# The residual of a one-core mLSTM / attention / expert block: loaded a second time and added by VectorE, and its products for the expert sums moved into the third expert group

## The chip, the cores and the metric

The kernel is one program on one core of a Trainium2 chip. The metric is the device time of one execution in microseconds (us), from a few timed runs; beside it stands one execution that the hardware profiler recorded, with its own time and its span (first to last instruction). TensorE is PE in the profile, VectorE DVE, ScalarE ACT, GpSimd POOL, SyncE SP. Each engine works through its own list of instructions in order and waits for others by semaphores.

## The reference

256 tokens of 1024 numbers go through one block: a mixer (an mLSTM group and a differential attention group), then 32 experts of which each token uses two, then a last norm. What matters here are the two residual sums:

```python
def reference(x, w_in, ..., w_out, norm1_g, norm2_g, ..., w_eg, w_eu, w_ed, normf_g):
    h = rmsnorm(x, norm1_g[l])
    proj = h @ w_in[l]
...
    x = x + jnp.concatenate([y_m, y_d.astype(x.dtype)], axis=-1) @ w_out[l]
    h2 = rmsnorm(x, norm2_g[l])
    x = x + hier_moe(h2, w_rg[l], b_rg[l], w_re[l], b_re[l], w_eg[l], w_eu[l], w_ed[l])
    return rmsnorm(x, normf_g)
```

`hier_moe` picks a group and two experts in it for each token by the logits of h2, and adds `gates * ((silu(t @ w_eg) * (t @ w_eu)) @ w_ed)` over the experts. The sum after `w_out` is called x1 below.

## The kernel before, in words

**Stages.** The first 150 us compute the mixer: projections with `w_in`, the recurrence, the attention, then the product with `w_out`, the router's logits and the list of experts. From there on the kernel runs ten groups of experts (a fixed four, then pairs and fours in the order of their load), `for pr in range(LAST)` at L1028, and one last group by hand. The expert weights are 32 x 6 MB in pieces of 1 MB.

**Weights and their places.** `order` lists 23 places (slots) of 1 MB in turn: six that the mixer also uses (`wa`), eleven that open when the mixer's tiles are closed (`wbs`, after `bx.close()`), six more at the other end of the memory (`wzs`). `load` (L877) sends a group's pieces on SP's queue; a piece waits until its slot's last reader is done, which for the first round means the mixer's tiles that lay there, and for the eighth transfer before it. From the seventh piece of `w_ed` on, a piece's expert is read out of `permi`, the order of the experts by load, which is known only when the router is done.

**The accumulators.** `acc[j][t]` are four banks of PSUM of 512 columns, j for the half of the 1024 columns and t for the half of the tokens. They take x1 and then all expert results (`scatter`, L845), and are read by the last norm.

**The stage around the change.** With `acc` open, TensorE first multiplies the residual into it, by the identity (L573 to L575):

```python
for j in range(2):
    for t in range(NT):
        T.matmul(acc[j][t], ident, xs[:, t, j * 512:(j + 1) * 512], start=True, stop=False, skip_group_check=True)
```

`xs` is x as the kernel loaded it at the start, one tile under the slots `wbs`. Then come eight steps k with three products for each half of the tokens: `wh` and `wl` are the high and the low part of a 128-row piece of `w_out`, made by ScalarE (L232) and VectorE (L233); `yH` and `yL` are those of the mixer's output (L566 and L567 for the mLSTM half, from `tm`, L565; L533 and L534 for the attention half). `cols` cuts the 1024 columns into blocks of 512, 256 and 256. Out of every 256 columns (a quarter, i) the kernel makes `x1` in the on-chip memory (L621, copies out of `acc`, one by VectorE and one by ScalarE), its squares (L628), its transposes (L638, L640) and the router's products (L647), whose logits VectorE adds up in `lg` (L652, L654). `keep_x1` (L592) keeps x1 for the experts' gathers in `x1c`, in an order (k, q) of the columns that fits the experts' weights.

What stands in which order on an engine is set by a scheduler with a timeline model of its own; `issue_after` and `high_priority` are hints to it.

Of the kernel before, what the change touches and what calls it, by code (L numbers as in the profile page):

```python
# [10 lines left out]
F32 = mybir.dt.float32  # L11
# [5 lines left out]
OP = mybir.AluOpType  # L17
AX = mybir.AxisListType

P = 128  # L20
S = 256
NT = 2
D = 1024
KD = 8
# [80 lines left out]
def kernel(ctx: ExitStack, tc: tile.TileContext,  # L105
# [467 lines left out]
    for j in range(2):  # L573
        for t in range(NT):
            T.matmul(acc[j][t], ident, xs[:, t, j * 512:(j + 1) * 512], start=True, stop=False, skip_group_check=True)  # L575

# [15 lines left out]
    def keep_x1(j, after):  # L592

        with tc.issue_after(after.ins):
            for t in range(NT):
                A.copy(x1c[:, t, :, j * 64:(j + 1) * 64],
                       acc[j][t].rearrange("p (q k) -> p k q", k=KD))
# [3 lines left out]
    for b, (c0, nc_) in enumerate(cols):  # L601
# [6 lines left out]
        for n, k in enumerate((4, 5, 6, 7, 0, 1, 2, 3) if b else (4, 5, 0, 1, 2, 3, 6, 7)):  # L608
            wh, wl = split(wo[2 * j + 1 - k // 4][:, k % 4, cs], rooms[n % 4] if b else two(n))
            for t in range(NT):  # L610
                ts = slice(t * P, (t + 1) * P)
                T.matmul(po[t], yH[:, k, ts], wh, start=False, stop=False, skip_group_check=True)  # L612
                T.matmul(po[t], yL[:, k, ts], wh, start=False, stop=False, skip_group_check=True)  # L613
                T.matmul(po[t], yH[:, k, ts], wl, start=False, stop=(n == KD - 1), skip_group_check=True)  # L614
        for i in range(c0 // 256, (c0 + nc_) // 256):
# [3 lines left out]
            x1 = px1.tile([P, NT, 256], F32, name="x1", tag="x1", bufs=2)  # L619
            for t in range(NT):  # L620
                (A.copy if t else V.tensor_copy)(x1[:, t], po[t])  # L621
# [33 lines left out]
            if i == 1:  # L655
                keep_x1(0, ev)
    keep_warm(NW2, pw, pe)
    if dbg is not None:
        for j in range(2):
            for t in range(NT):  # L660
                SY.dma_start(dap(dbg, t * P * D + j * 512, [[D, P], [1, 512]]), x1[j][:, t])
# [8 lines left out]
    keep_x1(1, behind[0])  # L670
# [174 lines left out]
    def scatter(n, S_, oj, j, stop=False):  # L845
        for o_ in halves(n, oj):
            for t in range(NT):
                T.matmul(acc[j][t], S_[:n, t * P:(t + 1) * P], o_[:n], start=False, stop=stop, skip_group_check=True)  # L848
# [182 lines left out]
    for pr in range(LAST):  # L1031
# [6 lines left out]
        for j, oj in enumerate(down(ws, hT, [po2(), po2()])):  # L1038
            scatter(P, S_, oj, j)
# [168 lines left out]
```

## Time and profile before

| | us |
|---|---|
| median of 3 runs | 592.17 (590.98 to 594.12) |
| the profiled execution's own time | 594.47 |
| its span | 592.7 |
| PE, DVE, ACT, POOL busy in it | 517.1, 158.2, 122.5, 9.4 |
| mean granted clock of TensorE | 0.955 of full speed |
| moved by DMA | 223.76 MB, mean 378 GB/s |

The profiled execution took 2.3 us more than the median of the runs, and its span leaves 1.8 us of its own time outside. Times of the trace count from the start of the span. A busy PE is not PE at its peak, since products that follow each other overlap in the records; the distance between two starts is the better measure there.

### The profile page before, as it was taken

To read this page: it belongs to the slowest core of one execution; us is meant where nothing else is said; L and a number is where in the kernel's file an instruction comes from. 1 tells how busy PE (TensorE), PEld (TensorE's weight loads), DVE (VectorE), ACT (ScalarE), POOL (GpSimd) and SP (SyncE) were. 2 spreads that over 40 slices of the span, in tenths; PEclk is the share of its full clock that TensorE was granted. 3 is DMA by queue.
4 is the path that set the end of the run, shared out by engine and by line. 5 is a ranking of instruction groups with operands and counts; after the bars stand their busy time and mean duration, and the time that the engine had idled before them with its cause. 6 is when DMAs were issued, how large, how long until landed. Compare 5 with 4: busy or idle time off the path is not lost.

```text
span 592.7 us, 7989 instructions
## 1 busy us (share of the span) xinstructions
PE 517.1 (87%) x3004; PEld 263.5 (44%) x3004; DVE 158.2 (27%) x463; ACT 122.5 (21%) x287; POOL 9.4 (2%) x19
## 2 busy tenths in 40 slices
PE   8999999999969999799897897995897986885783
PEld 6898879796353343334242252341243331221130
DVE  3784688946031120201102002001002002000022
ACT  4775568663011000000100000000010000000032
POOL 0000002201000000000000000000000000000000
PEclk9999999999969999999799998999999989899798
DMA  8964799998999999999999999999999999999991
GB/s 292 390 190 112 225 387 382 322 343 346 388 420 417 421 417 421 419 418 421 419 420 418 421 418 421 419 419 420 420 420 420 419 420 419 420 419 421 399 346 73
DMA packets 49019, 223.76 MB, mean 378 GB/s; under 512 B 3796, under 2 KB 6228, under 8 KB 27348
## 3 DMA queue, kind: packets, MB, share of 16 engines
q1 hardware_dynamic: 48692, 222.89, 94.6%
q8 instruction: 24, 0.39, 0.3%
q10 hardware_dynamic: 288, 0.35, 0.2%
q14 instruction: 15, 0.12, 0.1%
HBM read 221.39 MB, written 1.84 MB: 377 GB/s over the span
## 4 chain that ended last, share of the span: by engine, by line
PE 48%; DMA 46%; DVE 3%; ACT 1%; issue 1%; SPq 0%; ACTq 0%
DMA w<-in_w_ed_dram 18%; DMA w<-in_w_eu_dram 17%; PE pmm L906 11%; DMA w<-in_w_eg_dram 10%; PE pmm L923 7%; PE pmm L815 4%; PE pj L264 3%; PE pj L261 3%; PE pj L263 3%; PE acc L848 1%; PE pj L274 1%; PE pj L275 1%; PE acc L612 1%; PE pj L273 1%; PE acc L613 1%; PE acc L614 1%
## 5 line engine op out<-in xcount | busy, mean ns | idle before, releaser
L906 PE MATMUL pmm<-w,xg 128*32 128x512 f32 (+1 forms) x1024 | 189.8, 615 | 24.2 <-DMA w<-in_w_eu_dram 16.0
L906 PEld LDWEIGHTS pmm<-w,xg 128*32 128x32 f32 (+1 forms) x1024 | 47.0, 118 | 139.1 <-issue 89.9
L923 PE MATMUL pmm<-w,oL 128*32 128x512 f32 (+1 forms) x448 | 93.9, 673 | 11.8 <-ACT oL L835 6.1
L923 PEld LDWEIGHTS pmm<-w,oL 128*32 128x32 f32 (+1 forms) x448 | 27.9, 130 | 72.2 <-issue 45.9
L233 DVE TENSOR_TENSOR wl<-w,wh 128x512 fp32r<-128x512 f32 (+1 forms) x72 | 44.5, 629 | 24.4 <-ACT wh L232 21.7
L842 DVE TENSOR_TENSOR oL<-pmm,oH 128x512 fp32r<-128x512 f32 x18 | 12.4, 691 | 134.3 <-PE pmm L923 111.3
L815 PEld LDWEIGHTS pmm<-Gm,x1c 128*128 128x128 f32 x320 | 39.9, 204 | 16.5 <-issue 8.9
L815 PE MATMUL pmm<-Gm,x1c 128*128 128x128 f32 x320 | 43.0, 293 | 4.7 <-DVE beg L997 4.7
L232 ACT ACTIVATE wh<-w 128x512 fp32r<-128x512 f32 (+1 forms) x72 | 41.0, 581 | 29.5 <-PE pj L263 13.7
L263 PE MATMUL pj<-hL,wh 128*128 128x256 f32 x128 | 36.9, 292 | 0.0
L261 PE MATMUL pj<-hH,wh 128*128 128x256 f32 x128 | 36.2, 294 | 0.0
L264 PE MATMUL pj<-hH,wl 128*128 128x256 f32 x128 | 36.1, 293 | 0.0
L835 ACT COPY oL<-pmm 128x512 f32<-128x512 f32 x9 | 5.3, 586 | 139.0 <-PE pmm L832 139.0
L841 ACT CAST oH<-pmm 128x512 fp32r<-128x512 f32 x18 | 10.6, 586 | 112.8 <-PE pmm L923 92.7
L816 DVE TENSOR_TENSOR xg<-pmm,cb 128x512 f32<-128x512 f32 (+1 forms) x22 | 13.5, 639 | 68.3 <-PE pmm L906 51.9
L263 PEld LDWEIGHTS pj<-hL,wh 128*128 128x128 f32 x128 | 25.1, 196 | 0.1
L264 PEld LDWEIGHTS pj<-hH,wl 128*128 128x128 f32 x128 | 24.5, 195 | 1.4 <-issue 1.2
L261 PEld LDWEIGHTS pj<-hH,wh 128*128 128x128 f32 x128 | 24.7, 196 | 0.2
L832 PE MATMUL pmm<-ca,oH 128*128 128x128 f32 x40 | 6.9, 300 | 18.7 <-DVE oH L828 18.7
L913 ACT ACTIVATE oL<-pmm,rg 128x512 f32<-128x512 f32 x9 | 6.2, 688 | 80.3 <-PE pmm L906 62.9
L832 PEld LDWEIGHTS pmm<-ca,oH 128*128 128x128 f32 x40 | 4.7, 152 | 26.1 <-issue 23.6
L613 PE MATMUL acc<-wh,yL 128*128 128x256 f32 (+1 forms) x48 | 15.1, 322 | 0.0
(337 smaller groups left out, 476.0 us busy)
## 6 DMA issues: line engine op xcount, KB each, us to landing
w<-in_w_eu_dram SPq DMA_DIRECT2D x64, 1024.0 KB, 19.8
w<-in_w_eg_dram SPq DMA_DIRECT2D x64, 1024.0 KB, 19.8
w<-in_w_ed_dram SPq DMA_DIRECT2D x56, 1024.0 KB, 19.8
w<-in_w_in_dram SPq DMA_DIRECT2D x10, 1024.0 KB, 14.6
w<-in_w_ed_dram SPq DMA_DIRECT2D x12, 512.0 KB, 13.6
w<-in_w_out_dram SPq DMA_DIRECT2D x4, 1024.0 KB, 12.8
w<-in_w_ed_dram SPq DMA_DIRECT2D x8, 256.0 KB, 7.4
w<-in_w_in_dram SPq DMA_DIRECT2D x3, 512.0 KB, 8.2
```

Of the source, the lines that this page charges most:

```text
L232: A.activation(wh, raw, AF.Copy)
L233: V.tensor_tensor(wl, raw, wh.bitcast(F32), op=OP.subtract)
L261: T.matmul(om, wh[:, cs], hH[:, k], start=(k == 0 and m % 2 == 0), stop=False, skip_group_check=True)
L263: T.matmul(om, wh[:, cs], hL[:, k], start=False, stop=False, skip_group_check=True)
L264: T.matmul(om, wl[:, cs], hH[:, k], start=False, stop=(k == KD - 1), skip_group_check=True)
L613: T.matmul(po[t], yL[:, k, ts], wh, start=False, stop=False, skip_group_check=True)
L815: gat_end[0] = T.matmul(px_[:, i * P:i * P + n], x1c[:, t, k0 + i], G_[:, t], start=(t == 0), stop=(t == NT - 1))
L816: V.tensor_tensor(xg[:, k0:k0 + per, :n], px_.rearrange("p (k s) -> p k s", k=4)[:, :per, :n], cb[:, B_N2 + k0:B_N2 + k0 + per, None].to_b ...
L832: T.transpose(pt[:, k * P:k * P + n], hid[:n, k], ident[:n, :n])
L842: V.tensor_tensor(oL[:n], oj[:n], oH[:n].bitcast(F32), op=OP.subtract)
L906: up_end[0] = T.matmul(p_[i * cap:(i + 1) * cap], xg[:, k, i * cap:(i + 1) * cap], of(ws, n_, i, k), start=(k == 0), stop=(k == KD - 1))
L923: down_end[0] = T.matmul(ojs[j][i * cap:(i + 1) * cap], hT[:, k, i * cap:(i + 1) * cap], ws["d", i, k // 2][:, c0:c0 + 512], start=(k == 0 ...
```

## The change

The four products of the residual into `acc` are gone; the first product of `w_out` now starts each bank. Each quarter of x comes from memory a second time, 256 KB by a DMA on GpSimd's queue, into the tile that `x1` uses (two of them in turn; the third load waits until the first quarter is used up). VectorE adds the bank to it, for both halves of the tokens. `keep_x1` now copies each quarter out of `x1` rather than each half out of `acc`. As `acc` holds no residual any more when the experts begin, the first group's first product starts it anew, and behind the third group's scatters (`pr == 2`) four products of `x1c` with the identity bring x1 in.

```diff
     acc = [[pacc.tile([P, 512], F32, name=f"acc{j}{t}") for t in range(NT)] for j in range(2)]
-    for j in range(2):
-        for t in range(NT):
-            T.matmul(acc[j][t], ident, xs[:, t, j * 512:(j + 1) * 512], start=True, stop=False, skip_group_check=True)
-
     bx.close()
...
-    def keep_x1(j, after):
+    def keep_x1(i, x1, after):
 
         with tc.issue_after(after.ins):
             for t in range(NT):
-                A.copy(x1c[:, t, :, j * 64:(j + 1) * 64],
-                       acc[j][t].rearrange("p (q k) -> p k q", k=KD))
+                A.copy(x1c[:, t, :, i * 32:(i + 1) * 32], x1[:, t].rearrange("p (q k) -> p k q", k=KD))
+
+    def load_x1(i):
+
+        x1 = px1.tile([P, NT, 256], F32, name="x1", tag="x1", bufs=2)
+        G.dma_start(x1, dap(x, i * 256, [[D, P], [P * D, NT], [1, 256]]))
+        return x1
+
+    x1s = [load_x1(i) for i in range(2)]
...
-                T.matmul(po[t], yH[:, k, ts], wh, start=False, stop=False, skip_group_check=True)
+
+                T.matmul(po[t], yH[:, k, ts], wh, start=(n == 0 and cj == 0), stop=False, skip_group_check=True)
...
-            x1 = px1.tile([P, NT, 256], F32, name="x1", tag="x1", bufs=2)
+            x1 = x1s[i]
             for t in range(NT):
-                (A.copy if t else V.tensor_copy)(x1[:, t], po[t])
+                V.tensor_tensor(x1[:, t], x1[:, t], po[t], op=OP.add)
...
-            if i == 1:
-                keep_x1(0, ev)
+            if not last:
+                keep_x1(i, x1, ev)
+                if i < 2:
+                    x1s.append(load_x1(i + 2))
...
-    keep_x1(1, behind[0])
+    keep_x1(3, x1s[3], behind[0])
...
+    def residual():
+
+        for j in range(2):
+            for t in range(NT):
+                T.matmul(acc[j][t], ident, x1c[:, t, :, j * 64:(j + 1) * 64].rearrange("p k q -> p q k"),
+                         start=False, stop=False, skip_group_check=True)
...
         for j, oj in enumerate(down(ws, hT, [po2(), po2()])):
-            scatter(P, S_, oj, j)
+            scatter(P, S_, oj, j, pr == 0)
+        if pr == 2:
+            residual()
```

The scheduler also moves other instructions. On VectorE, in the first block of `w_out` (`tm`, `yL` are the mixer's output, `wl` the low part of `w_out`, `cT` the mLSTM's output before its gate, `l` the attention's), before:

```order
L565 TENSOR_TENSOR tm<-cT,zs 128x256 x2
L522 TENSOR_SCALAR l<-pm,rso 128x128 x4
L567 TENSOR_TENSOR yL<-tm,yH 128x256 x2
L565 TENSOR_TENSOR tm<-cT,zs 128x256
L233 TENSOR_TENSOR wl<-w,wh 128x512
L567 TENSOR_TENSOR yL<-tm,yH 128x256
L550 SCALAR_TENSOR_TENSOR cT<-pm,ca,cT 128x256
```

and now:

```order
L565 TENSOR_TENSOR tm<-cT,zs 128x256 x2
L522 TENSOR_SCALAR l<-pm,rso 128x128 x4
L233 TENSOR_TENSOR wl<-w,wh 128x512
L550 SCALAR_TENSOR_TENSOR cT<-pm,ca,cT 128x256
L567 TENSOR_TENSOR yL<-tm,yH 128x256
L233 TENSOR_TENSOR wl<-w,wh 128x512
L567 TENSOR_TENSOR yL<-tm,yH 128x256
L534 SCALAR_TENSOR_TENSOR yL<-pm,ca,yH 128x512
L565 TENSOR_TENSOR tm<-cT,zs 128x256 x2
L233 TENSOR_TENSOR wl<-w,wh 128x512
L567 TENSOR_TENSOR yL<-tm,yH 128x256
L233 TENSOR_TENSOR wl<-w,wh 128x512
```

The first two `yL` stood right behind L522 and the third one four rows later; now two and four rows come ahead of the first two, and nine operations behind L522 ahead of the third. On VectorE in the third quarter (`x_1642` before and `x_1555` now are its `x1`, `lg` the router's logits of the quarters ahead of it), before:

```order
L652 COPY lg<-pm 128x80
L621 COPY x_1642<-acc_1397 128x256
L233 TENSOR_TENSOR wl<-w,wh 128x256
L654 TENSOR_TENSOR lg<-lg,pm 128x80
L640 COPY x1T<-pm 128x256
```

and now:

```order
L656 COPY lg<-pm 128x80
L233 TENSOR_TENSOR wl<-w,wh 128x256
L658 TENSOR_TENSOR lg<-lg,pm 128x80
L625 TENSOR_TENSOR x_1555<-x_1555,acc_1397 128x256
L625 TENSOR_TENSOR x_1555<-x_1555,acc_1398 128x256
L644 COPY x1T<-pm 128x256
```

The third quarter's `x1` now stands behind the addition of the second quarter's logits, and it is two rows of VectorE where one was VectorE's and one ScalarE's. On SP, where the list of experts is first read (`TENSOR_LOAD permi` brings an expert's number into a register of SP), before:

```order
L770 DMA w<-in_w_ed_dram 128x2048 x6
L768 TENSOR_LOAD permi
L768 ISA x2
L770 DMA w<-in_w_ed_dram 128x2048
L768 TENSOR_LOAD permi
L768 ISA x2
L770 ISA
L770 DMA w<-in_w_eg_dram 128x2048
```

and now:

```order
L772 DMA w<-in_w_ed_dram 128x2048 x6
L770 TENSOR_LOAD permi
L770 ISA x2
L770 TENSOR_LOAD permi
L770 ISA x2
L772 DMA w<-in_w_ed_dram 128x2048
L770 TENSOR_LOAD permi
L770 ISA x2
L770 TENSOR_LOAD permi
L770 ISA x2
L772 ISA
L772 DMA w<-in_w_eg_dram 128x2048
```

Two reads stand ahead of the next transfer where one stood, and two more ahead of the one behind it.

## Rows read from the trace of the kernel before

**Rows 1.** Chain that ended last: start, us, what; its last transfer.

```profile
558.49 9.06 DMA w<-in_w_ed_dram
```

**Rows 2.** Stretches: us; PE, PEld, DVE, ACT, POOL busy; clock; DMA share; GB/s.

```profile
104.00:110.00 6.00, 5.83 (x34) 4.19 (x34) 5.67 (x18) 4.46 (x11) 4.04 (x5) 1.00 0.68 219
...
130.00:138.00 8.00, 7.60 (x66) 7.45 (x65) 3.12 (x9) 4.32 (x13) 0.00 (x0) 1.00 0.66 198
...
150.00:152.00 2.00, 2.00 (x27) 0.53 (x19) 0.00 (x0) 0.00 (x0) 0.00 (x0) 1.00 0.86 209
...
160.00:550.00 390.00, 334.97 (x1816) 129.28 (x1810) 47.20 (x109) 23.99 (x38) 0.00 (x0) 0.95 1.01 420
```

**Rows 3.** Waits of SP's queue, 60 to 165 us: us in total, times, longest.

```profile
SPq L768 <- DVE permf L966: 7.9, 1, 7.9
SPq L770 <- DVE wl L233: 7.7, 1, 7.7
```

**Rows 4.** Timeline of PE, first block of w_out: start, us, line, operation.

```profile
107.46 3.60 PE L575 MATMUL acc<-xs,ca 128*128 128x512 f32 x8
110.50 1.02 PE L612 MATMUL acc<-wh,yH 128*128 128x512 f32 x2
...
122.08 0.61 PE L614 MATMUL acc<-wl,yH 128*128 128x512 f32 x2
122.54 0.28 PE L612 MATMUL acc<-wh,yH 128*128 128x256 f32 x1
```

**Rows 5.** Timeline of VectorE in the same block.

```profile
112.02 0.75 DVE L567 TENSOR_TENSOR yL<-tm,yH 128x256 fp32r<-128x256 f32 x2
...
113.02 0.69 DVE L233 TENSOR_TENSOR wl<-w,wh 128x512 fp32r<-128x512 f32 x1
113.63 0.42 DVE L567 TENSOR_TENSOR yL<-tm,yH 128x256 fp32r<-128x256 f32 x1
114.07 0.48 DVE L550 SCALAR_TENSOR_TENSOR cT<-pm,ca,cT 128x256 f32<-128x256 f32 x1
114.47 0.68 DVE L233 TENSOR_TENSOR wl<-w,wh 128x512 fp32r<-128x512 f32 x1
```

**Rows 6.** Timelines of ACT, PE and DVE: quarters one to three on their way.

```profile
126.10 0.57 ACT L640 COPY x1T<-pm 128x512 f32<-128x512 f32 x1
...
129.28 0.63 PE L638 MATMUL pm<-ca,x 128*128 128x128 f32 x4
...
129.95 0.59 ACT L640 COPY x1T<-pm 128x512 f32<-128x512 f32 x1 [0.86 <-PE pm L638]
...
130.55 0.44 PE L638 MATMUL pm<-ca,x 128*128 128x128 f32 x2 [0.40 <-DVE x L621]
...
131.90 0.98 PE L647 MATMUL pm<-wrg,x1T 128*128 128x40 f32 x8
...
132.92 0.24 DVE L654 TENSOR_TENSOR lg<-lg,pm 128x80 f32<-128x80 f32 x1 [2.09 <-PE pm L647]
```

**Rows 7.** DMA issues: queue, count, KB each, median us to landing.

```profile
w<-in_w_ed_dram SPq DMA_DIRECT2D x56, 1024.0 KB, 19.8
...
w<-in_w_ed_dram SPq DMA_DIRECT2D x8, 256.0 KB, 7.4
...
xs<-in_x_dram SPq DMA_DIRECT2D x4, 256.0 KB, 6.2
...
out_dram<-w SPq DMA_DIRECT2D x3, 256.0 KB, 2.2
```

**Rows 8.** Line 768 on SP's queue: ns least/median/most, first and last start.

```profile
L768 SPq TENSOR_LOAD <-permi x28: 263/268/473, 148.6 to 179.1; - x28
L768 SPq FUSED_REGOPS  x28: 147/152/181, 149.2 to 179.4; - x28
```

**Rows 9.** Waits of SP's queue, 255 to 300 us (the third group).

```profile
SPq L770 <- PE pmm L923: 0.6, 2, 0.4
```

**Rows 10.** Line 621, x1 out of acc, on VectorE.

```profile
L621 DVE COPY x<-acc x4: 416/424/425, 122.5 to 138.5; 128x256 f32<-128x256 f32 x4
```

More of the change, by code (lines that the diff above doesn't have):

```diff
@@ L654 @@
                 V.tensor_tensor(lg, lg, pv, op=OP.add)
-            if i == 1:
-                keep_x1(0, ev)
+            if not last:
+                keep_x1(i, x1, ev)
+                if i < 2:
+                    x1s.append(load_x1(i + 2))
     keep_warm(NW2, pw, pe)
[L658 to L661, printed above, removed]
     def sm(name, n, dt=F32, pool=py):
@@ L843, in halves, with scatter @@
         return oH, oL
-    def scatter(n, S_, oj, j, stop=False):
-        for o_ in halves(n, oj):
+    def scatter(n, S_, oj, j, first=False):
+        oH, oL = halves(n, oj)
+        for o_ in (oH, oL):
             for t in range(NT):
-                T.matmul(acc[j][t], S_[:n, t * P:(t + 1) * P], o_[:n], start=False, stop=stop, skip_group_check=True)
+                T.matmul(acc[j][t], S_[:n, t * P:(t + 1) * P], o_[:n], start=first and o_ is oH, stop=False,
+                         skip_group_check=True)
+    def residual():
[3 more added lines that the diff above has]
+                         start=False, stop=False, skip_group_check=True)
     def one_hot(js):
```

## The prediction

> **What bounds the kernel now.** I read the chain of waits first. It ends in transfers of expert weights: the last is in at 567.6 us [rows 1], and 25 us of tail follow that the change doesn't touch. Then the stretches. From 160 to 550 us the DMA engines are never idle (share 1.01 at 420 GB/s), and TensorE is not what they wait for [rows 2]. So the end moves only with the bytes that are still to come and with time in which the DMA engines idle. Such time is found ahead of 160 us alone: a share of 0.68 in 104 to 110 us, 0.66 in 130 to 138 and 0.86 in 150 to 152 [rows 2]. Against 1.01 that is 2.0, 2.8 and 0.3 us. Third, SP's waits, for what those holes are made of: one of 7.7 us for VectorE's last split of a piece of w_out, whose place in memory the next transfer takes, and one of 7.9 us for the list of experts [rows 3]. Both end with the w_out stage. So the question is when that stage ends, and what the extra bytes and SP's own steps do to the holes.
>
> **TensorE's four products, gone from 107 us.** Each is recorded as two. The first starts at 107.46, the first product of w_out at 110.50 [rows 4], so 3.04 us of a TensorE that has no gap there fall away. That would bring 3.04 us if w_out's inputs were there, but the new order on VectorE takes most of it back. Behind L522, which ends at 112.02, it does a wl (steps of 0.61), a cT (0.40), a yL (0.38, half of 0.75), a wl, a yL, the attention's yL (twice 0.38), two tm (0.38 each) and a wl before the third yL of 0.42 [rows 5]. That sums to 0.61 x 3 + 0.40 + 0.38 x 6 + 0.42 = 4.9 us, so the third yL is there at 116.9; before, it was there at 114.05 [rows 5]. Behind it TensorE has 22 products of 512 columns left in this block, at a step of 0.23 us (two of them in 0.46 [rows 4]): 5.1 us, end at 122.0. Before, the block ended at 122.54 [rows 4]. **Gain here: 0.5 us** of the 3.04. If the inputs were no bound it is 3.0; a loss has no reason here, since nothing was added to TensorE. One transfer that waited for the last of these products can go earlier; the DMA engines have enough in their queues there until the hole at 130, so this buys nothing.
>
> **The third quarter.** Its x1 now waits for the second quarter's logits, as VectorE does them first. Before, that quarter's transposes ran from 129.28 to 129.91; 0.5 earlier is 129.4. Copying them out takes 0.59, the router's products 0.98 and the addition 0.24 [rows 6]: 131.2, and the first addition of the third quarter (priced as the copy that it replaces, 0.42 [rows 10]) ends at 131.6. TensorE stands behind it with the third quarter's transposes, which started at 130.55 before [rows 6], 1.05 us earlier. But the second quarter's router products, 0.98, then lay behind that point and lie ahead of it now. So the stage ends 0.1 us later, at 138.6 (before: the last copy's start, 138.5 [rows 10]): **no change**. Bounds: 0.9 earlier, if that addition isn't late, to 1.1 later.
>
> **The loads.** No DMA runs on GpSimd's queue before, so their time is bounded: 256 KB land in 2.2 us where nothing else moves, in 6.2 us for x at the start, in 7.4 us behind others of its own queue; 1 MB in a full queue takes 19.8 [rows 7]. The first two are issued behind GpSimd's last work on hn, about where w_out's block starts, and are used at that block's end: covered by some 12 us [rows 4]. The third can start only when ScalarE has copied the first quarter into x1c: its x1T copy was at 126.10 and is at 125.6 now, 0.57 long [rows 6], then two copies of half the width, some 0.4 each: 127.0. It is used at 131.2, so the cover is 4.2 us. Its own queue is empty; of the 7.4 us some 5 are the seven pieces of 0.6 us ahead of it on the same queue. I take 3.5 us, nearer to the 2.2 than to the 6.2, and so **nothing**; 6.2 costs 2.0 us, one for one on the stage's end. The fourth starts near 131 and is used at 138.5: covered by 7 us. The Trainium skill, "DMA: Bandwidth & Descriptors", section "Queues, rings and completion order", has each DMA engine take turns between the queues that have work, packet by packet; by that rule the third load doesn't wait for the 1 MB pieces that SP has queued, which agrees with the value taken, though no row here shows two busy queues.
>
> **Their bytes.** 1.05 MB at 420 GB/s are 2.5 us of DMA time. The hole at 130 to 138 us holds 2.8 us, and three of the four loads fall ahead of their end, so the queue only runs dry later: I take **nothing**, upper bound 2.5.
>
> **The tail of the stage.** Both additions of the last quarter now stand on VectorE in a row, where one copy each was on two engines: 0.42 for the second one [rows 10], of which the transposes of the first half hide a little: **+0.3** until the list of experts is known.
>
> **SP.** Of the reads of the list one more stands ahead of the first transfer behind it. Each is 0.27 + 0.15 us [rows 8]: **+0.4**. The DMA engines are at the end of their work just then (share 0.86 [rows 2]), so this delays the stream. The other added read stands behind a 1 MB transfer (2.5 us) and is hidden.
>
> **The third group.** The four products come back there, 3.04 us, and read x1c in a strided order that no row prices. They lie under transfers: SP waited for TensorE for 0.6 us in all in that stretch [rows 9], and a piece lands 19.8 us after its issue at 2.5 us each [rows 7], so some eight are in flight. **Nothing**; without that cover 3.0. `keep_x1` copies the same numbers as before.
>
> **Sum.** 0 (stage) + 0 (loads, bytes) + 0.3 + 0.4 + 0 = +0.7 us. The profiled execution would go from 594.47 to 595.2; it lies 2.3 over the median of the runs shown, so for the median I forecast 592.17 + 0.7 = **592.9 us**.
>
> **Rivals.**
> *The products' time comes through.* If VectorE's new order isn't the bound, the stage ends 3.0 us earlier and the list too: -3.04 + 0.7 = -2.3, 589.8 us. For it: TensorE has no gap there. Against it: the nine rows ahead of the third yL. Even this stays within 0.5% (3 us, which is about what a measurement of this kernel tells from no change).
> *The bytes are paid.* The kernel is bound by its transfers, so 1.05 MB more are 2.5 us more, unless a hole takes them: 0.7 + 2.5 = +3.2, 595.4 us. For it: the share of 1.01 to the end. Against it: a hole of 2.8 us just where the loads fall. It decides where the loads come after 138 us or the hole has closed before they come.
> *The third load lands late* (the one that ends on the other side). TensorE stands in order behind the third quarter's transposes, then so do w_out's last products, the router and SP. Landing at L us costs L - 131.2. At 6.2 us +2.0, in all 594.9; from 6.5 us on it is slower by over 0.5%; behind the pieces queued by SP, at the 19.8 us row, 146.8 and +15.6, 608 us. For it: no row shows this queue, and the start waits for two ScalarE copies. Against it: an empty queue of its own. The Trainium skill, "SBUF — State Buffer", section "Who interferes with whom", says that GpSimd writes such a load's descriptors and is shut out while VectorE copies or scales within the on-chip memory in its fast modes. By the trace VectorE does splits (two inputs) and a copy out of PSUM there, and the page's list has neither for such a block; its price of some 2.5 us would put the landing of 3.5 us at 6.0.
> *The cover in the third group fails:* +3.0, in all +3.7, 595.9 us. Against it stand eight transfers of 2.5 us each in flight.
>
> **How the numbers follow.** Forecast (stage unchanged to 1 us either way, the third load up to 2 us late): 0.60. Products come through: 0.13. Bytes paid: 0.10. Third load late by more than 2 us: 0.11. Third group: 0.06. Faster by over 0.5% needs more than the -2.3 of the best case and the runs' own spread (590.98 to 594.12): 0.06. Slower: the late load, half each of the bytes and of the group, 0.11 + 0.05 + 0.03, 0.19. Same: 0.75. The range reaches from the best case, 589.8, to the group's case and a third load that is 3.5 us late, 596.4; it leaves out later loads and the runs' spread beyond it, 2 in 10.
>
> **What would show it.** L575's rows gone and w_out's first product near 107.5; a gap on TensorE near 112 to 116.9 that waits for yL; its block end near 122.0; the third quarter's transposes near 131.6, behind the second's router products, waiting for VectorE's addition and that for `lg`, not for the DMA; the stage's end within 1 us of 138.5; the share in 130 to 138 us up by a fifth to a third; the first transfer by the list 0.5 to 1 us later; 160 to 550 us full as before. The prediction is wrong if the additions of the third quarter wait for x, if the stage ends before 137 or after 141, or if the share stays low while the loads move.

## The result and the profile after

The changed kernel takes 598.39 us in the median of 10 runs (595.76 to 603.11), the kernel before 591.62 on the same chip (590.30 to 594.17). The ratio is 1.0118, with an interval of 1.0099 to 1.0137: slower by 1.2%, some 7 us. The forecast was 592.9, with a range up to 596.4. The runs of the changed kernel are also spread wider than those of before (7.4 us against 3.9).

The profiled execution of the changed kernel took 596.55 us (span 594.2), near the quickest of its runs, and that of before 594.47, slower than any of the ten runs it is compared with. In the trace of after w_out's stage begins 2.7 us earlier than in that of before, in code that the change doesn't touch; in the other traces below it begins anywhere from 104.2 to 107.2 us. So I compare the stage by its own start, and judge kernels by the ratios of their runs.

Busy time and the queue of the new loads, from the page of after:

```profile
PE 514.7 (87%) x3004; PEld 259.8 (44%) x3004; DVE 158.7 (27%) x467; ACT 123.7 (21%) x287; POOL 12.5 (2%) x23
...
q0 software_dynamic: 320, 1.05, 0.5%
```

No engine's sum has moved by more than 3.1 us (GpSimd's, which now issues the four loads), and the sums don't show the loss. The timeline of PE does (start, us, operation; in brackets the idle time ahead of it and what ended that):

```profile
104.76 0.97 PE L616 MATMUL acc<-wh,yH 128*128 128x512 f32 x2
...
110.87 0.50 PE L617 MATMUL acc<-wh,yL 128*128 128x512 f32 x1 [0.76 <-DVE yL L567]
...
119.19 0.28 PE L616 MATMUL acc<-wh,yH 128*128 128x256 f32 x1
...
127.25 1.08 PE L651 MATMUL pm<-wrg,x1T 128*128 128x40 f32 x8 [0.44 <-ACT x1T L644]
131.25 0.66 PE L642 MATMUL pm<-ca,x 128*128 128x128 f32 x2 [2.91 <-DVE x L625]
...
132.13 0.41 PE L618 MATMUL acc<-wl,yH 128*128 128x256 f32 x1
132.34 0.41 PE L616 MATMUL acc<-wh,yH 128*128 128x256 f32 x1
...
136.02 0.28 PE L617 MATMUL acc<-wh,yL 128*128 128x256 f32 x1
136.14 0.28 PE L618 MATMUL acc<-wl,yH 128*128 128x256 f32 x1
```

The first block takes 119.19 - 104.76 = 14.43 us; before, 122.54 - 107.46 = 15.08 [rows 4]. That is a gain of 0.65 us, where 0.5 was forecast. Then, ahead of the third quarter's transposes, TensorE stands idle for 2.91 us, where it waited 0.40 before [rows 6]. Behind that wait its products of 256 columns start 0.21 us apart and not 0.12, until about 135.8. Why it waited is on ScalarE, GpSimd and VectorE, one row of each timeline after the other:

```profile
123.12 1.26 ACT L592 COPY x1c<-x 128x256 f32<-128x256 f32 x2
124.68 0.72 POOL L597 DMA_DIRECT2D x<-in_x_dram  x1 [17.64 <-PE acc L617]
128.37 0.24 DVE L658 TENSOR_TENSOR lg<-lg,pm 128x80 f32<-128x80 f32 x1 [1.03 <-PE pm L651]
130.73 0.75 DVE L625 TENSOR_TENSOR x<-x,acc 128x256 f32<-128x256 f32 x2 [2.12 <-DMA x<-in_x_dram]
...
140.45 0.75 DVE L625 TENSOR_TENSOR x<-x,acc 128x256 f32<-128x256 f32 x2 [2.04 <-PE acc L618]
```

ScalarE is done with the first quarter's copies at 124.38, GpSimd issues the third load at 124.68, and VectorE's addition, which has its logits out of the way at 128.6, waits until 130.73 for that load. The profile names a product of w_out (PE, L617) as what ended GpSimd's idle time, but no such product reads the buffer; of its readers ScalarE's copies are done last. The run below in which ScalarE issues this load itself bears that out: there it leaves 0.04 us behind the copies. The issues of the loads, and SP's waits from 60 to 165 us:

```profile
x<-in_x_dram POOLq DMA_DIRECT2D x4, 256.0 KB, 7.1
```

```profile
SPq L772 <- DVE wl L233: 19.0, 3, 10.6
```

256 KB land in 7.1 us in the median; the third load is used 130.73 - 124.68 = 6.0 us behind its issue. SP's longest wait for the last splits of w_out is 10.6 us now and was 7.7 [rows 3]. The stretches (the last three columns: TensorE's granted clock, share of the DMA engines, GB/s):

```profile
104.00:110.00 6.00, 5.48 (x26) 3.60 (x24) 5.90 (x20) 5.84 (x12) 3.04 (x4) 1.00 0.92 314
...
120.00:128.00 8.00, 7.56 (x66) 7.36 (x64) 3.95 (x11) 7.05 (x20) 0.72 (x1) 1.00 1.04 397
128.00:130.00 2.00, 0.34 (x4) 0.22 (x2) 0.24 (x1) 0.30 (x1) 0.72 (x1) 0.74 1.07 387
130.00:132.00 2.00, 0.75 (x4) 0.78 (x5) 0.75 (x2) 0.77 (x4) 0.00 (x0) 0.50 1.02 409
132.00:134.00 2.00, 2.00 (x11) 2.00 (x11) 0.00 (x0) 0.14 (x2) 0.00 (x0) 0.50 0.64 248
134.00:136.00 2.00, 2.00 (x12) 2.00 (x11) 0.42 (x1) 1.07 (x3) 0.00 (x0) 0.55 0.18 73
136.00:138.00 2.00, 2.00 (x20) 2.00 (x19) 1.17 (x5) 1.72 (x5) 0.00 (x0) 1.00 0.09 33
138.00:150.00 12.00, 10.56 (x77) 7.35 (x75) 8.36 (x51) 3.33 (x15) 1.74 (x6) 1.00 0.87 326
150.00:152.00 2.00, 2.00 (x22) 0.76 (x25) 0.62 (x3) 0.00 (x0) 0.00 (x0) 1.00 1.03 434
152.00:154.00 2.00, 2.00 (x24) 0.53 (x19) 0.00 (x0) 0.00 (x0) 0.00 (x0) 1.00 0.88 291
...
156.00:158.00 2.00, 2.00 (x19) 0.99 (x12) 0.00 (x0) 0.00 (x0) 0.00 (x0) 1.00 0.83 315
...
160.00:550.00 390.00, 335.88 (x1818) 127.53 (x1810) 47.23 (x109) 23.98 (x38) 0.00 (x0) 0.96 1.01 420
```

The clock is at the lower of its two levels (0.50, 1.2 of 2.4 GHz) from about 129.0 to 135.8 us; before, it stayed at 1.00 in 130 to 138 us [rows 2]. From 104 to 110 us the share is 0.92, where it was 0.68 [rows 2]: the first two loads fill a hole. Later the DMA engines run dry: shares of 0.64, 0.18 and 0.09 from 132 to 138 us, and 0.87 behind that. From 160 to 550 us all is as before, 1.01 and 420 GB/s. So what the trace shows of the loss lies ahead of 160 us, in the w_out stage and what follows from it.

Its length, from the first product in `acc` to VectorE's square of the last quarter (L625 before, L629 in the changed kernel, which starts at 141.12), is 36.36 us after and 138.97 - 107.46 = 31.51 before: 4.85 us more in these two executions. What the DMA engines moved in the 65 us from that start on says the same (before, then after):

```profile
107.46:172.46 65.00, 58.10 (x415) 40.17 (x414) 32.79 (x124) 24.89 (x70) 2.32 (x7) 0.96 0.96 367
```

```profile
104.76:169.76 65.00, 57.49 (x402) 39.65 (x401) 30.92 (x119) 24.87 (x69) 5.46 (x11) 0.95 0.91 348
```

That is 23.86 MB before and 22.62 after, of which 1.05 are the new loads: 2.28 MB behind, 5.4 us at 420 GB/s. The medians differ by some 7 us, and the traced execution is one of the quicker ones; what more the slower executions lose, no trace shows.

**Theory.** The third load can start only when ScalarE has copied the first quarter out of one of the two buffers, and lands about 7 us later. TensorE waits for it, its clock falls behind the wait, the last splits of w_out come later for both reasons, and SP's transfers with them. **Rivals:** the 1.05 MB themselves; GpSimd's queue as the reason why the landing takes so long; VectorE's additions and the copies by quarters; the third group's products.

### The profile page after: what moved, and what is told of

It is laid out like the page before. It is cut to its first block, busy times and chain, and to the rows that moved or that the text cites. A ratio compares the mean times of both kernels' runs of the same rounds, so it can differ in the third digit from the quotient of the medians.

```text
span 594.2 us, 8021 instructions
## 1 busy us (share of the span) xinstructions
PE 514.7 (87%) x3004; PEld 259.8 (44%) x3004; DVE 158.7 (27%) x467; ACT 123.7 (21%) x287; POOL 12.5 (2%) x23
## 3 DMA queue, kind: packets, MB, share of 16 engines
q0 software_dynamic: 320, 1.05, 0.5%
## 4 chain that ended last, share of the span: by engine, by line
DMA 47%; PE 46%; DVE 3%; ACT 2%; issue 1%; SPq 0%; POOLq 0%; ACTq 0%
DMA w<-in_w_ed_dram 21%; DMA w<-in_w_eu_dram 13%; PE pmm L917 12%; DMA w<-in_w_eg_dram 10%; PE pmm L934 7%; PE pmm L817 4%; PE pj L264 3%; PE pj L263 2%; PE pj L261 2%; PE acc L851 2%; PE pj L274 1%; PE pj L275 1%; PE pj L273 1%; DMA xs<-in_x_dram 1%; DMA x<-in_x_dram 1%
## 5 line engine op out<-in xcount | busy, mean ns | idle before, releaser
L934 PE MATMUL pmm<-w,oL 128*32 128x512 f32 (+1 forms) x448 | 86.0, 638 | 11.1 <-ACT oL L837 6.1
L934 PEld LDWEIGHTS pmm<-w,oL 128*32 128x32 f32 (+1 forms) x448 | 24.9, 125 | 66.4 <-issue 43.6
L817 PEld LDWEIGHTS pmm<-Gm,x1c 128*128 128x128 f32 x320 | 38.7, 198 | 18.1 <-issue 10.6
L843 ACT CAST oH<-pmm 128x512 fp32r<-128x512 f32 x18 | 10.6, 586 | 104.2 <-PE pmm L934 84.2
L617 PE MATMUL acc<-wh,yL 128*128 128x256 f32 (+1 forms) x48 | 16.0, 342 | 1.2 <-DVE yL L567 0.8
L616 PE MATMUL acc<-wh,yH 128*128 128x256 f32 (+1 forms) x48 | 15.8, 352 | 0.0
## 6 DMA issues: line engine op xcount, KB each, us to landing
w<-in_w_eu_dram SPq DMA_DIRECT2D x64, 1024.0 KB, 19.8
w<-in_w_eg_dram SPq DMA_DIRECT2D x64, 1024.0 KB, 19.8
w<-in_w_ed_dram SPq DMA_DIRECT2D x56, 1024.0 KB, 19.8
```

The source lines that it names most:

```text
L616: T.matmul(po[t], yH[:, k, ts], wh, start=(n == 0 and cj == 0), stop=False, skip_group_check=True)
L817: gat_end[0] = T.matmul(px_[:, i * P:i * P + n], x1c[:, t, k0 + i], G_[:, t], start=(t == 0), stop=(t == NT - 1))
L934: down_end[0] = T.matmul(ojs[j][i * cap:(i + 1) * cap], hT[:, k, i * cap:(i + 1) * cap], ws["d", i, k // 2][:, c0:c0 + 512], start=(k == 0 ...
```

## The experiments

Each ratio is to the kernel before on the same chip. Together they give this table; the stage is measured as above, the wait is TensorE's ahead of the third quarter's transposes, and the time at the lower clock is worked out from the 2 us stretches of 128 to 142 us as (1 - clock) / 0.5 of each. "Bytes late" is how far the DMA engines are behind those of before 65 us from the stage's start, worked out as above.

| kernel | ratio | interval | stage | wait | lower clock | bytes late |
|---|---|---|---|---|---|---|
| before | | | 31.51 | 0.40 | 0 | |
| changed | 1.0118 | 1.0099 to 1.0137 | 36.36 | 2.91 | 6.8 | 5.4 |
| third load held longer (e7) | 1.0165 | 1.0147 to 1.0183 | 41.55 | 7.86 | 10.2 | 9.2 |
| loads 3, 4 on ScalarE's queue (e5) | 1.0129 | 1.0112 to 1.0146 | 36.08 | 3.34 | 3.4 | 5.9 |
| wait filled with products (e3) | 1.0088 | 1.0072 to 1.0104 | 34.27 | 0.29 | 0 | 3.3 |
| copies earlier (e8) | 1.0070 | 1.0048 to 1.0092 | 35.87 | 1.71 | 6.8 | 3.9 |
| three buffers (e2) | 1.0033 | 1.0016 to 1.0050 | 31.21 | 0.40 | 0 | 0.6 |
| three, the third apart (e9) | 1.0033 | 1.0018 to 1.0047 | 31.23 | 0.40 | 0 | -0.1 |

One thing differs between these kernels besides: how many reads of the list of experts SP puts ahead of the first transfer that needs it. The first read and that transfer in the trace of after, and the transfer in that of before:

```profile
L770 SPq TENSOR_LOAD <-permi x28: 262/268/480, 150.7 to 182.2; - x28
```

```profile
152.16 0.34 SPq L772 DMA_DIRECT2D w<-in_w_ed_dram  x1
```

```profile
149.53 0.34 SPq L770 DMA_DIRECT2D w<-in_w_ed_dram  x1
```

The transfer leaves 1.5 us behind the first read here and 0.9 before (the read was at 148.6 [rows 8]). It is 1.5 with ScalarE's queue too and 1.1 with the copies earlier, but 0.9 where the wait is filled, where the load is held longer, and in both kernels with three buffers. So some 0.5 us between two ratios can be SP's; the stage's length holds none of it.

**Three buffers (e2).** The wait is taken away by taking away what makes it:

```
-        x1 = px1.tile([P, NT, 256], F32, name="x1", tag="x1", bufs=2)
+        x1 = px1.tile([P, NT, 256], F32, name="x1", tag="x1", bufs=3)
...
-    x1s = [load_x1(i) for i in range(2)]
+    x1s = [load_x1(i) for i in range(3)]
...
-                if i < 2:
-                    x1s.append(load_x1(i + 2))
+                if i < 1:
+                    x1s.append(load_x1(i + 3))
```

> The changed kernel with three x1 buffers in place of two: the third load of x is issued with the first two at about 105 us and waits for nobody; the fourth waits for ScalarE's copies of the first quarter, with some 10 us of cover. Bytes, additions, copies and the four products of the third group stay. Late-load theory (TensorE waits for the third quarter's load, its clock falls, and the DMA engines stay empty for as long): no wait for x in the third quarter, granted clock 1.00 from 130 to 138 us, from the first product of w_out to the last addition some 30.5 us where the changed kernel takes 35.7; ratio 0.996 to 1.004. Bytes rival (1.05 MB at 420 GB/s, 2.5 us, paid in full): ratio 1.004 to 1.006 and the same without the wait. Rival that the additions on VectorE, the copies by quarters or the third group's products are the cost: the ratio stays at 1.009 to 1.014.

Measured: 593.09 us, ratio 1.0033 (1.0016 to 1.0050). Of PE's timeline, and of the stretches:

```profile
127.99 0.63 PE L642 MATMUL pm<-ca,x 128*128 128x128 f32 x4
...
129.25 0.44 PE L642 MATMUL pm<-ca,x 128*128 128x128 f32 x2 [0.40 <-DVE x L625]
...
130.49 0.98 PE L651 MATMUL pm<-wrg,x1T 128*128 128x40 f32 x8
```

```profile
130.00:132.00 2.00, 2.00 (x21) 2.00 (x19) 0.24 (x1) 1.27 (x5) 0.00 (x0) 1.00 1.04 377
132.00:134.00 2.00, 2.00 (x21) 2.00 (x19) 0.42 (x1) 1.72 (x4) 0.00 (x0) 1.00 1.08 422
```

The wait is back at the 0.40 us of before, the clock stays at 1.00, and the stage is 0.3 us shorter than before (31.21; some 30.5 had been expected). The scheduler also puts the third quarter's transposes ahead of the second's router products again, as in the kernel before. One edit takes away 0.85 of the 1.18%, up to 0.1 of it by SP's order. The additions, the loads and the third group's products are all still there, so together they hold what is left, 0.33%. That is the upper end of the 0.996 to 1.004 expected of the late load, and its interval reaches into the bytes' 1.004 to 1.006, so the bytes needed a run of their own.

**The wait filled (e3).** The wait stays, but TensorE has something to do in it:

```
                     x1s.append(load_x1(i + 2))
+                if i == 1:
+                    keep_warm(12, pw, pe)
```

> The changed kernel with 12 products of the kernel's own filling kind (their result is read by nobody) behind the second quarter's router products, where TensorE stands idle for 2.9 us waiting for the third load. The wait stays as it is. Late-load theory with the clock as a part of it: granted clock 1.00 in place of 0.50 from 130 to 136 us, the third and fourth quarter's products 0.12 us apart where they are 0.21 us apart now, some 2 us given back, ratio 1.006 to 1.010. If the wait alone is the cost, and the clock's fall lies beside something else: 1.010 to 1.014, no change against the changed kernel. Bytes rival: no change either.

Measured: 595.61 us, 1.0088 (1.0072 to 1.0104). PE's timeline and two stretches:

```profile
128.85 2.76 PE L189 MATMUL pm<-warm 128*128 128x512 bf16 x12
131.91 0.41 PE L642 MATMUL pm<-ca,x 128*128 128x128 f32 x2 [0.29 <-DVE x L625]
...
132.27 0.28 PE L617 MATMUL acc<-wh,yL 128*128 128x256 f32 x1
132.39 0.28 PE L618 MATMUL acc<-wl,yH 128*128 128x256 f32 x1
```

```profile
130.00:132.00 2.00, 1.71 (x9) 0.66 (x8) 0.62 (x2) 0.11 (x1) 0.01 (x1) 1.00 1.06 405
132.00:134.00 2.00, 2.00 (x18) 2.00 (x19) 0.17 (x2) 0.80 (x4) 0.00 (x0) 1.00 0.88 341
```

The transposes start as late as before the edit, 26.4 us behind the first product (131.91 - 105.48) against 26.5, but the products behind them are 0.12 us apart. In the stage this gives back 36.36 - 34.27 = 2.1 us, and as much in the bytes. In the ratio it is 0.0030 (1.8 us); the two intervals just overlap, and with both halves, 0.0019 and 0.0016, in quadrature the difference is 0.0005 to 0.0055. Some 0.5 us of it can be SP's order. So work that nobody reads makes the stage shorter, and the runs go the same way. The clock's fall is a part of the loss by itself, and the wait alone, against three buffers, is worth 34.27 - 31.21 = 3.1 us of the stage and 0.0055 (3.3 us).

**The other queue (e5).**

```
-        G.dma_start(x1, dap(x, i * 256, [[D, P], [P * D, NT], [1, 256]]))
+        (A if i > 1 else G).dma_start(x1, dap(x, i * 256, [[D, P], [P * D, NT], [1, 256]]))
```

> The changed kernel with the third and the fourth load issued from ScalarE's queue in place of GpSimd's; they still wait for the copies that free the buffers. If the 6 to 8 us from issue to landing come from GpSimd's own queue: landing under 4 us, TensorE's wait under 1 us, clock 1.00, ratio 0.998 to 1.004. If they come from the weights' transfers that fill the same engines (the 256 KB transfers of x ahead took 6.2 us from SP's queue): landing 5 to 8 us, wait 2 to 4 us, ratio 1.008 to 1.016. The late-load theory allows both; the bytes rival says the same ratio as the changed kernel whatever the landing.

Measured: 597.95 us, 1.0129 (1.0112 to 1.0146). Issues, the third load from ScalarE, and PE:

```profile
x<-in_x_dram POOLq DMA_DIRECT2D x2, 256.0 KB, 7.2
x<-in_x_dram ACTq DMA_DIRECT2D x2, 256.0 KB, 7.2
```

```profile
123.88 0.39 ACTq L597 DMA_DIRECT2D x<-in_x_dram  x1
```

```profile
131.14 0.66 PE L642 MATMUL pm<-ca,x 128*128 128x128 f32 x2 [3.34 <-DVE x L625]
```

7.2 us from either queue, and the third load is used 6.7 us behind its issue from ScalarE's queue (123.88 to 130.62), where it was 6.0 from GpSimd's: GpSimd is not the reason. What remains is that the loads share the DMA engines with SP's pieces, at a share of 1.04 in 120 to 128 us, here as in the changed kernel. That is argued from this share; no run takes those pieces away.

**Held longer, twice (e6, e7).** The first try placed the third load behind the second quarter's copies in the order alone, with three buffers:

```
+                if i == 1:
+                    with tc.issue_after(ev.ins):
+                        x1s += [load_x1(2), load_x1(3)]
```

> The changed kernel with three buffers, but the third and the fourth load held back until ScalarE has copied the second quarter's transposed x1 (127.2 us in the changed kernel, where the third load was issued at 124.7): the suspected wait made longer by some 2.5 us, with the same bytes and the same work. Late-load theory: TensorE waits 5 to 6 us in the third quarter in place of 2.9, the end moves by as much, ratio 1.015 to 1.022. Bytes, additions or third-group rivals: 1.009 to 1.014 as the changed kernel.

Measured: 592.42 us, 1.0021 (1.0010 to 1.0033). The load wasn't held: GpSimd issues three loads in a row in this trace, from 111.97. As an experiment on the wait it failed; it is a second run of three buffers, and agrees with the first. The next holds the load by a dependence (the fourth load, which waits for less, goes ahead of it):

```
+    def load_x1(i, hold=None):
...
+        x1 = px1.tile([P, NT, 256], F32, name="x1", tag="x1", bufs=3)
+        if hold is not None:
+            A.copy(x1[:, 0, :2], hold)
...
+                if i == 1:
+                    with tc.issue_after(ev.ins):
+                        x1s += [load_x1(2, x1T[:, 0, :2]), load_x1(3)]
```

> The changed kernel with three x1 buffers, where the third load is held back by a dependence: ScalarE writes two numbers of its buffer from the second quarter's transposed x1 (copied until 127.2 us in the changed kernel), and only then may the load go, some 2.7 us later than in the changed kernel (124.7). Bytes and the other work stay. Late-load theory: TensorE waits 5 to 6 us in the third quarter in place of 2.9, its clock falls again, and the ratio goes from 1.012 to 1.014 to 1.020. If the load's lateness is not what costs: 1.002 to 1.005, as with three buffers and no wait.

Measured: 601.59 us, 1.0165 (1.0147 to 1.0183), in the middle of what was expected. GpSimd, VectorE and PE:

```profile
128.85 0.72 POOL L599 DMA_DIRECT2D x<-in_x_dram  x1 [3.29 <-ACT x L598]
135.82 0.75 DVE L627 TENSOR_TENSOR x<-x,acc 128x256 f32<-128x256 f32 x2 [7.06 <-DMA x<-in_x_dram]
136.35 0.66 PE L644 MATMUL pm<-ca,x 128*128 128x128 f32 x2 [7.86 <-DVE x L627]
```

Counted from the stage's start (104.89 here), the load is issued 4.0 us later than in the changed kernel and used 5.0 us later, and the stage is 5.2 us longer. The clock is low for 10.2 us here. The wait of 7.86 is more than the 5 to 6 expected, since the load left 1.3 us later than reckoned, behind the second quarter's own x1c copies.

**Copies earlier (e8).** Two buffers, but `keep_x1` stands right behind the additions:

```
             for t in range(NT):
-                V.tensor_tensor(x1[:, t], x1[:, t], po[t], op=OP.add)
+                ad = V.tensor_tensor(x1[:, t], x1[:, t], po[t], op=OP.add)
+            if not last:
+                keep_x1(i, x1, ad)
...
-            if not last:
-                keep_x1(i, x1, ev)
-                if i < 2:
-                    x1s.append(load_x1(i + 2))
+            if i < 2:
+                x1s.append(load_x1(i + 2))
```

> The changed kernel with its two buffers, but ScalarE makes the x1c copies of a quarter right behind the additions, ahead of its squares and of the copy of the transposes, so that the third load waits for the first quarter's transposes alone (122.5 us) and goes some 2 us earlier. Late-load theory: TensorE's wait for x in the third quarter falls from 2.9 to about 1 us, with a shorter stretch at the lower clock or none, ratio 1.004 to 1.009. A rival, that 1.3 us of copies in front of the splits of w_out hold TensorE up as much: 1.010 to 1.014.

Measured: 596.28 us, 1.0070 (1.0048 to 1.0092). PE, and two stretches:

```profile
131.17 0.66 PE L644 MATMUL pm<-ca,x 128*128 128x128 f32 x2 [1.71 <-DVE x L625]
```

```profile
134.00:136.00 2.00, 2.00 (x11) 2.00 (x11) 0.70 (x2) 0.81 (x3) 0.00 (x0) 0.50 0.25 100
136.00:138.00 2.00, 2.00 (x16) 2.00 (x16) 1.32 (x4) 1.23 (x3) 0.00 (x0) 0.76 0.14 47
```

The ratio is in the range, and the wait is shorter, but in this execution the clock falls all the same and is low for 6.8 us. So the stage is only 0.5 us shorter than in the changed kernel, though the wait is 1.2 shorter; the bytes are 1.5 us less late, and the runs gain 0.0048 (2.8 us). The stage alone understates this gain. The third load left at 123.99, 18.4 us behind the first product against 19.9, later than hoped: the copies were done at 122.29, and the profile names the second quarter's addition on VectorE as what GpSimd waited for then.

**The third apart (e9).** Where the bytes fall:

```
+    x1b = px1.tile([P, NT, 256], F32, name="x1b", tag="x1b")
...
+        x1 = x1b if i == 2 else px1.tile([P, NT, 256], F32, name="x1", tag="x1", bufs=2)
...
+    x1s = [load_x1(i) for i in range(3)]
```

> Three buffers, of which the third lies apart and takes the place that is freed last (at 112 us, by the products that read an earlier tile there), so that the first two loads go at 105 us, where the DMA engines are not full, and not at 112.6, as with three buffers in one piece. Bytes theory of what is left with three buffers (ratio 1.0033 and 1.0021 in two runs): DMA share from 104 to 110 us at 0.85 or more in place of 0.70, ratio down by up to 0.002, to 1.000 to 1.002. If what is left are the additions, the copies by quarters or the third group's products: no change, 1.002 to 1.004.

Measured: 593.00 us, 1.0033 (1.0018 to 1.0047). The first two loads did leave earlier, at 107.81 and not 112.59, but the share in 104 to 110 us was 0.75, not 0.85, so the test is weak. Nothing was gained.

**The bytes alone (e10).** Added to the kernel before:

```
+    for i in range(4):
+        x1b = px1.tile([P, NT, 256], F32, name="x1b", tag="x1b")
+        G.dma_start(x1b, dap(x, i * 256, [[D, P], [P * D, NT], [1, 256]]))
```

> The kernel before, plus the four loads of 256 KB of x from GpSimd's queue into one buffer that nobody reads, one after the other from about 112 us. Nothing else is changed. If what is left with three buffers is the price of the bytes: ratio 1.002 to 1.005. If it is the additions, the copies or the third group's products: 0.999 to 1.001. Bytes rival for the whole loss: 1.009 or more.

Measured: 591.98 us, 1.0007 (0.9992 to 1.0023), and a stage of 31.52 us as before. By the interval the bytes cost 1.4 us at most, where 2.5 were the price in full.

**The third group (e11).** From e9, with x1 left out of the experts' sum:

```
-        if pr == 2:
-            residual()
```

> Three buffers with the third apart (ratio 1.0033, no wait for a load), without the four residual products of the third group: x1 is left out of the experts' sum. In the changed kernel these products took 0.87 us for each of their eight records, some 7 us of TensorE in all, where 0.38 us each had been reckoned. If they lie hidden behind the weights' transfers (DMA share 1.01 around them): no change, ratio 1.002 to 1.0045. If they are what is left over with three buffers: 0.999 to 1.0015.

Measured: 592.91 us, 1.0028 (1.0008 to 1.0049), against 1.0033 with them: they are hidden, to within some 1.8 us (the intervals, 0.0021 and 0.0015, in quadrature, less the difference). They are far dearer than reckoned, though, as two rows of PE's timeline in the changed kernel's trace show (a product is recorded as two; the group of their line gives 1.04 us for one record, and that of L575 0.59 before):

```profile
260.07 3.62 PE L858 MATMUL acc<-x1c,ca 128*128 128x512 f32 x4
...
268.23 3.62 PE L858 MATMUL acc<-x1c,ca 128*128 128x512 f32 x4
```

Four records take 3.62 us, a step of (3.62 - 1.04) / 3 = 0.86 us; before, eight of 0.59 us took 3.60 [rows 4], a step of (3.60 - 0.59) / 7 = 0.43.

**The copies by quarters (e12).** In the kernel before:

```
-                (A.copy if t else V.tensor_copy)(x1[:, t], po[t])
+                V.tensor_copy(x1[:, t], po[t])
...
-            if i == 1:
-                keep_x1(0, ev)
+            if not last:
+                keep_x1(i, x1, ev)
```

> The kernel before, with its products at the start and no loads, but x1 taken from the accumulators by VectorE alone (two copies a quarter where VectorE and ScalarE share them) and x1c copied by quarters from x1. If VectorE's serial work and the copies by quarters are what is left over with three buffers: ratio 1.002 to 1.004. If not: 0.999 to 1.0015.

Measured: 592.28 us, 1.0023 (1.0002 to 1.0045), stage 31.84. Slower, by something between 0.1 and 2.7 us.

**The first block without the products (e13).** The kernel before without x in the first sum:

```
-    for j in range(2):
-        for t in range(NT):
-            T.matmul(acc[j][t], ident, xs[:, t, j * 512:(j + 1) * 512], start=True, stop=False, skip_group_check=True)
...
-                T.matmul(po[t], yH[:, k, ts], wh, start=False, stop=False, skip_group_check=True)
+                T.matmul(po[t], yH[:, k, ts], wh, start=(n == 0 and cj == 0), stop=False, skip_group_check=True)
```

> The kernel before without the four products of x at the start of the first block: the residual is left out. Step of the prediction that VectorE's order holds the block, so that 0.5 of the 3.04 us come through: from the first product of w_out to the first of the second block some 14.4 to 14.6 us (15.08 with the products), ratio 0.998 to 1.000. If all of the 3 us come through: 0.994 to 0.9955.

Measured: 590.30 us, 0.9976 (0.9959 to 0.9993). The block takes 119.32 - 104.86 = 14.46 us, 0.62 less than before, and the stage 0.59 less. The ratio is just under the expected 0.998 to 1.000. All of the 3.04 us is ruled out; by the runs the gain is 0.4 to 2.4 us.

**An attempt at a better kernel (e14).** No loads; the products are moved into the places where TensorE waits for VectorE in that block, with the pools that need x's room behind them:

```
+            if b == 0 and n == 2:
+                for jj in range(2):
+                    for t in range(NT):
+                        T.matmul(acc[jj][t], ident, xs[:, t, jj * 512:(jj + 1) * 512], start=jj == 1, stop=False, skip_group_check=True)
+
+                bx.close()
...
```

> The kernel before with its four products of x moved from the start of the first block into the places where TensorE waits there for VectorE: two behind the first two products of w_out, two behind the second row block's. No loads, no new additions; x's first copy stays in SBUF some 4 us longer. If the block without these products is held by VectorE (14.46 us from its first product to the second block's in place of 15.08, ratio 0.9976 with the residual left out), most of the 0.6 us of the block comes through: ratio 0.997 to 0.9995. If the products only push what follows them: 0.9995 to 1.001. If the weights' transfers wait for the room that x holds longer: above 1.001.

Measured: 591.17 us, 0.9993 (0.9976 to 1.0011): no change that can be told. The block takes 120.28 - 104.87 = 15.41 us, longer than the 15.08 of before, and the stage 31.86. No kernel with the whole computation that I ran is shown to beat the one before.

## Why the prediction was wrong, point by point

**The step that failed: "I take 3.5 us, nearer to the 2.2 than to the 6.2, and so nothing".** From its issue to its use the third load measured 6 to 7 us in every kernel that waited for it: 6.0 in the changed one, 6.7 from ScalarE's queue, 7.0 where it was held. So it was 2.1 us late, where the sum had nothing. The start was right (19.5 us behind the block's start were reckoned, 19.9 came), and so was the cover: 4.2 us reckoned; the addition was free 128.6 - 124.68 = 3.9 us behind the issue. The bound that was written down, x's own 6.2 us [rows 7], was the better value, and it was put off with the argument that an empty queue lands sooner. The queue was empty, but the engines behind it were not (share 1.04). The 2.2 us that the value leaned on are stores (`out_dram<-w`) at the kernel's end; the quickest loads of this size in the trace of before, left out there, already took more than the 3.5:

```profile
w<-in_w_in_dram SPq DMA_DIRECT2D x2, 256.0 KB, 3.8
```

The Trainium skill, "DMA: Bandwidth & Descriptors", section "Queues, rings and completion order", says that an engine takes turns between queues. That a 256 KB load lands in 7 us where a 1 MB piece takes 19.8 agrees with it, as the load does not stand behind the pieces; that it costs little does not follow.

**What was missing: TensorE's clock.** The third rival, "the third load lands late", is what happened, but its price counted the wait one for one on the stage's end: 594.9 us at 6.2. The wait measured 2.5 us more than before (2.91 against 0.40), the stage 4.85 more. Filling the wait gave back 2.1 us in the stage, and the runs moved by 1.8 the same way, so most of what the wait itself doesn't hold is shown to be the clock. The rows say the same: 18 products of 256 columns start 0.21 us apart in place of 0.12, 18 x 0.09 = 1.6 us, and the transposes among them are slower too. The rival had a chance of 0.11, for a load more than 2 us late, while a load up to 2 us late was counted in the forecast; 2.1 us came, just past that line. By the prediction's own price this would have been some 595 us and within the range. What took the time out of the range is the clock's 2.1 us and, as far as the numbers add up, what three buffers still cost and a loss in the runs that the trace doesn't hold. (The 608 us at the 19.8 us row leave out the 0.7 of the other terms.)

**Queued to the end.** That the end moves with DMA idle time ahead of 160 us held: with the load held longer, the stage grew by 41.55 - 31.51 = 10.0 us, the bytes were 9.2 us late, and the median grew by 1.65% of 591.5, 9.8 us.

**"Gain here: 0.5 us of the 3.04".** Right in the block: 0.65 in the changed kernel, 0.62 where only this was done. TensorE's gap for yL (0.76) is where it was looked for, and the product that needs the third yL starts at 114.08, 9.3 us behind the block's first; 9.4 had been reckoned. In the runs that edit alone was worth 0.24% (1.4 us, interval 0.4 to 2.4).

**The third quarter's order.** As forecast, the transposes stood behind the second quarter's router products. But the addition waited for x, not for the logits, which is what the prediction named as its refutation. The share in 130 to 138 us, forecast to rise, fell to 0.48 from 0.66 [rows 2]. With the load early the order itself turned back, so that the forecast order was not the one that three buffers bring.

**ScalarE's copies** took 0.6 us each (the pair 1.26), where 0.4 was assumed. This moved the third load by some 0.4 us.

**The bytes: nothing, upper bound 2.5.** Right in size: 1.0007 for them alone.

**SP and the tail: +0.4 and +0.3.** SP's step came as reckoned: the first transfer by the list is 0.5 us further behind the first read. The hole behind it, which lay at 150 to 156 us before, is at 152 to 160 now: with shares of 0.88, 0.96, 0.83 and 0.96 it is 0.8 us against 1.01, and was 0.4 with 0.86, 0.97 and 0.99. From the last quarter's first operation on VectorE to that read it is 150.7 - 140.45 = 10.2 us, and was 148.6 - 138.5 = 10.1 [rows 8, rows 10], so the tail grew by less than the 0.3.

**The third group: hidden.** Right as far as the runs can tell, on wrong numbers: 8 steps of 0.86 us, some 7 us, lay there and not 3.04, and without them the ratio is the same within its interval. SP's waits were no cause there, as was reckoned from [rows 9].

**What stays open.** Three buffers still cost 0.2 to 0.3% (1.0021, 1.0033, 1.0033), though their stage is 0.3 us shorter than before. By single edits the bytes (+0.0007), the copies by quarters (+0.0023) and the products taken away (-0.0024) come to +0.0006, and each interval reaches 0.0015 to 0.0022 to either side, some 0.003 for the sum. So the rest, some 1.4 us, isn't placed, and by these intervals the three could also hold all of it. The forecast of +0.7 us for the kernel without a late load would have been low by about 1 us. Open too is why the changed kernel's runs lose some 2 us more than its trace, and are spread so wide.

## What to carry to other kernels

When a buffer is loaded again while it is still being copied out, work out the moment of the issue from the copy's end and price the landing by the slowest row of that size under a full set of DMA engines, not by the emptiness of the queue. A wait of TensorE in front of dense products may have to be charged for the wait and for the products behind it at half the clock, and filling it with idle products shows which part is which. One more buffer took the wait away here.

## What the runs showed of the hardware that was not expected

- In the run with earlier copies TensorE's granted clock fell to 0.50 within a wait of 1.71 us and stayed there for 6.8 us, though TensorE was busy again for some 5.8 us of it; with a wait of 3.34 us (ScalarE's queue) it was low for 3.4 us, and with one of 0.40 us it stayed at 1.00. In these runs the time at the lower clock did not go with the length of the wait. The Trainium skill, "TensorE: Matmul & The Clock Gate", section "What's actually happening", has the two levels as halved and full; the traces agree, with products of 256 columns 0.21 us apart at the one and 0.12 at the other.
- A 256 KB load took 7.2 us from GpSimd's and from ScalarE's queue alike, with SP's pieces in flight. The prediction cited a rule on GpSimd's descriptors being shut out (the Trainium skill, "SBUF — State Buffer", section "Who interferes with whom"); the loads that went from ScalarE's queue (GpSimd's carried 160 packets then, and not 320) landed no sooner, so it is not what made the third load late.
- The identity products of 512 columns took steps of 0.86 us where they read x1c in the order (q, k), whose neighbours lie 128 numbers apart, and 0.43 where they read x in a row before, with the clock at 1.00 in both. The Trainium skill, "SBUF — State Buffer", section "Door 1: The DMA port swizzle", says that each step to another 16-byte line of the memory costs time; this agrees, and no run here tells its price from that of another cause.
